# Modulation vectors by 32-column quarters of TensorE, four-block norms, and the residual affine after the first feed-forward products, in a two-block fp32 kernel

## The chip, the cores and the metric

The kernel runs on one core of one Trainium2 chip. The metric is the device time of one launch in microseconds (us), as the median of several runs. Engines are named as in the profile: PE is the matrix engine (TensorE), PEld its weight loads, DVE the vector engine, ACT the scalar engine, POOL the GpSimd engine, SP the engine that issues most transfers. `L253` is line 253 of the kernel before.

## The reference, cut to what matters

Two transformer-like blocks run one after the other on one sequence of 1024 tokens with 1024 features, all in fp32. The change touches the first block only:

```python
mod = silu(c) @ w_mod + b_mod          # 6 vectors of 1024: shift, scale, gate, twice
h   = x * (1 + scale1) + shift1        # 256 context tokens likewise, with c_ctx
y   = concat(mlstm(h), sgu(h), conv(h), s5(h)) @ w_out      # four mixers of 256 features
x1  = layer_norm(ALPHA * x + gate1 * y) * ln1_w + ln1_b
ff  = (silu(g) * u) @ w_ffn_out,  [g, u] = (x1 * (1 + scale2) + shift2) @ w_ffn_in
x2  = layer_norm(ALPHA * x1 + gate2 * ff) * ln2_w + ln2_b   # input of the second block
```

Two mixers end in a layer norm of their own over 256 features per token (the gated unit `sgu` and the convolution). The second block (attention, a state-space mixer and a linear recurrence) is the same in both kernels.

## The kernel before, in words

**Products.** Every large product is done in three passes: each fp32 operand is split into a rounded part `hi` and a rest `lo`, and hi*hi, hi*lo and lo*hi are added up in PSUM (`mm3` L237, `dense` L243, `tokens` L270). Weights come in chunks of 256 KB by `wpart` (L219): SP issues the load into `raw` (3 buffers), ACT copies `raw` to `whi` (L215), and DVE or POOL subtracts to `wlo` (L212). With a scale vector `wpart` first multiplies the chunk on DVE or POOL (L231); so is `w_out` multiplied by the gate `g0` and `w_ffn_out` by `g1`.

**Order of the work.** The kernel is written as generators that yield `(busy, wait)` estimates; `weave` (L146) runs some twenty of them side by side on a planned clock and so writes the program out in one order. Buffers come from pools of numbered slots (28 `u`, 7 `ub`, 5 `f` of 512 columns, 8 PSUM banks); `need` and `spare` make a generator wait on the planned clock until slots are free. `after(name)` waits until another generator has added that name. The tile framework then orders each engine's instructions by a timeline that it simulates itself (`schedule_with_timeline_sim=True`). At run time each engine works through its own queue in that order, and waits in a queue hold back all behind them.

**Stages of the first block.** (1) Start: `mod_part(st)` (L442) computes shift1 and scale1 for `c` and `c_ctx` in two steps, `st` 0 and 1, each for four of the eight feature blocks. Each step loads eight chunks of 512 KB of `w_mod` (L434) and multiplies them on PE with a stationary operand of 4 columns (L463, `128*4`); the chunks in `MSPLIT` are split into hi and lo first (tile `wms`), the others are used as fp32. The row of 512 sums goes to SBUF by DVE (`modrow` L469) and is turned into columns by PE (`pmt` L472). At the same time DVE builds tables for the s5 mixer (`s5_tables` L332). Then `h_split` (L482) makes the input of the projections. (2) The projections of `project` (L1363) run on PE, one after the other; beside them DVE does the 31 taps of the convolution (L823), the gates and the scans. (3) After the convolution, the other eight modulation vectors' halves are computed by `mod_part(n)` (L1300), `n` 0 and 1 for `g0`, 2 to 5 for the columns of shift2 and scale2, and 6 and 7 for `g1` after the name `wo0`. Each loads four chunks of 512 KB (L1312) and accumulates eight products of 512 columns on DVE into `macc` (L1325, L1327); PE then sums over the partitions (`pmr` L1334, or `pmb` L1342 as columns). (4) After the last projection come the second mLSTM pair, the second half of s5 in up to three streams (`s5_batch` L1133) and the norm of the convolution. (5) `out_proj` (L1451) multiplies by `w_out` in four groups of rows and halves; `norm_add` (L1501) adds the products to `res`, the residual, and takes statistics. (6) `norm1` (L1515) normalises two token blocks of 128 at a time: statistics, `rsqrt` (L292: 12 small DVE operations by Newton steps), `res` normalised in place (L1527), then `to_features` (L1479): PE transposes into PSUM, DVE scales and shifts into `hf` (L1493), ACT copies to hi and DVE subtracts to lo (L215 and L212, tile `h`). After all eight blocks, `norm1` loads `ln1` by POOL's queue and multiplies and adds it to `res` on POOL (L1548, L1549: 16 operations of 1024 columns), and names `res` done. (7) `feed_forward` (L1628) first runs three tiles of `ff_in` for the first half of the tokens, then for the second half; then tiles alternate with groups of `ff_out` (L1577), which needs the name `res`.

`ln2blocks` (L846) is the norm of two token blocks at once, with one `rsqrt` for both; `conv_norm` and `sgu_mixer` call it four times each.

Of the kernel before, what the change touches and what calls it, by code (L numbers as in the profile page):

```python
# [39 lines left out]
AFFV, LOV, SCG = 0, 2, 4  # L40
# [35 lines left out]
def tile_block(ctx: ExitStack, tc: tile.TileContext, A, out):  # L76
# [341 lines left out]
    cs = const.tile([128, 8, 4], F32, name="cs")  # L418
    s.activation(cs[:, :, 0], col("c", 0, 8), AF.Silu)
    s.activation(cs[:, :, 1], col("c_ctx", 0, 8), AF.Silu)  # L420
    v.memset(cs[:, :, 2:4], 0.0)
    cs4 = const.tile([128, 8, 4], F32R, name="cs4")
    v.tensor_copy(cs4[:, :, 0:2], cs[:, :, 0:2])
    v.tensor_tensor(cs4[:, :, 2:4], cs[:, :, 0:2], _r(cs4[:, :, 0:2]), op=ALU.subtract)
    fold = const.tile([4, 2], F32, name="fold")
    v.tensor_tensor(fold[:], ident[0:4, 0:2], ident[0:4, 2:4], op=ALU.add)
# [14 lines left out]

    def mod_part(st):  # L442
        items = [(n, q) for n in (st, 2 + st) for q in range(4)]
        todo = sorted((i + (MLAG if i in MSPLIT[st] else 0), i) for i in range(8))
        last = {i // 4: i for _, i in todo}
        pm, parts = {}, {}
        pmt = bank("pmt", (128, 8, 2))
        for pos, i in todo:
            for j in range(8):
                if j <= pos + 0.5 and j not in parts:  # L450
                    parts[j] = [wms[items[j]]]
                    if j in MSPLIT[st]:
                        yield from need(u=2)
                        parts[j] = [u("wms", (128, 2, 512), F32R) for _ in range(2)]
                        split(wms[items[j]][:], parts[j][0][:], parts[j][1][:], dve=j in MDVE[st])
                        free(wms[items[j]])
            n, q = i // 4, i % 4
            new = n not in pm
            if new:
                pm[n] = bank("pmod")  # L460
            for k in range(2):
                for x in parts[i]:
                    pe.matmul(pm[n][0:4, :], (cs4 if i in MSPLIT[st] else cs)[:, 2 * q + k, :], x[:, k, :],  # L463
                              start=new and k == 0 and x is parts[i][0],
                              stop=last[n] == i and k == 1 and x is parts[i][-1])
            free(parts[i])
            if last[n] == i:
                row = f512("modrow")
                v.tensor_copy(row[0:4, :], pm[n][0:4, :])  # L469
                free(pm[n])  # L470
                for c in range(4):
                    pe.matmul(pmt[:, 4 * n + c, :], row[0:4, c * 128:(c + 1) * 128], fold[:], start=True, stop=True)  # L472
                free(row)
            yield 0.86 if i in MSPLIT[st] else 1.72, 0.0
# [371 lines left out]
    def ln2blocks(ps_, xs, width):  # L846
        st = small("lnst", [128, 2, 6])
        mv = small("lnmv", [128, 2, 2])
        rs = small("lnrs", [128, 2])
# [4 lines left out]
        for j in range(2):  # L854
            v.tensor_scalar(xs[j], ps_[j], mv[:, j, 0:1], rs[:, j:j + 1], op0=ALU.subtract, op1=ALU.mult)

    def conv_norm():
        yield from after("cv0", "cv1", *GATE["n"])
        yield from need(u=4)
        cv = [load(f"cv{i}") for i in range(2)]  # L860
        xn = [u(f"cxn{q}", (128, 4, 256)) for q in range(2)]
        yield 0.0, 4.0
        for t in range(0, 8, 2):
            yield from need(ps=1)
            p = bank("pct", (128, 2, 256))
            for j in range(2):
                for i in range(2):
                    pe.transpose(p[:, j, i * 128:(i + 1) * 128], cv[i][:, (t + j) * 128:(t + j + 1) * 128], ident[:])
            ln2blocks([p[:, j, :] for j in range(2)], [xn[t // 4][:, t % 4 + j, :] for j in range(2)], 256)
# [192 lines left out]
    def sgu_mixer():  # L1062
# [16 lines left out]
        for t in range(0, 8, 2):  # L1079
            x = [vn[t // 4][:, t % 4 + j, :] for j in range(2)]  # L1080
            ln2blocks(x, x, 256)
            x = vn[t // 4][:, t % 4:t % 4 + 2, :]
            g.tensor_tensor(x, x, lnwb[:, 0, :].unsqueeze(1).to_broadcast([128, 2, 256]), op=ALU.mult)
            g.tensor_tensor(x, x, lnwb[:, 1, :].unsqueeze(1).to_broadcast([128, 2, 256]), op=ALU.add)
            yield 0.0, 3.0
# [214 lines left out]
    def mod_part(n):  # L1300
# [5 lines left out]
        yield from need(f=1)  # L1306
        acc = f512("macc")
        wms = []
        for q in range(5):
# [5 lines left out]
            if q:  # L1315
                wm = wms[q - 1]
                if q in MACP.get(n, ()):
                    for k in range(2):
                        s.activation(wm[:, k, :], wm[:, k, :], AF.Copy, scale=cs[:, 2 * q - 2 + k, 0:1])
                    g.tensor_tensor(wm[:, 0, :], wm[:, 0, :], wm[:, 1, :], op=ALU.add)  # L1320
                    v.tensor_tensor(acc[:], acc[:], wm[:, 0, :], op=ALU.add)
                for k in range(2) if q not in MACP.get(n, ()) else ():
                    kk = 2 * (q - 1) + k
                    if kk == 0:
                        v.tensor_scalar(acc[:], wm[:, k, :], cs[:, kk, 0:1], None, op0=ALU.mult)  # L1325
                    else:
                        v.scalar_tensor_tensor(acc[:], wm[:, k, :], cs[:, kk, 0:1], acc[:],  # L1327
                                               op0=ALU.mult, op1=ALU.add)
                free(wm)
        yield 0.0, 3.0  # L1330
# [148 lines left out]
    def to_features(xs, c0, X, hf, names, scale, bias, mul=None):  # L1479
        for d in range(0, 8, 2):  # L1480
# [5 lines left out]
            for e in range(2):  # L1486
# [28 lines left out]
    def norm1():  # L1515
        yield from after("mod")
        for un in range(4):
            if True:
                yield from after(f"wosum{un // 2 * 2 + 1}")
                mv = small("mv1", [128, 2, 2])  # L1520
                rs = small("rsd", [128, 2])
                ts = (2 * un, 2 * un + 1)
                for j, t in enumerate(ts):
                    v.bn_aggr(out=mv[:, j, :], in_=st1[:, t].rearrange("p a b -> p (a b)"))
                rsqrt(rs[:], mv[:, :, 1], 2, 1.0, LN_EPS)
                for j, t in enumerate(ts):
                    v.tensor_scalar(res[t][:], res[t][:], mv[:, j, 0:1], rs[:, j:j + 1],  # L1527
                                    op0=ALU.subtract, op1=ALU.mult)
                yield 0.0, 9.0
                hf = un // 2  # L1530
                if un % 2 == 0:
                    for d in range(8):
                        yield from need(u=1)
                        H2[d, hf] = u("h2", (128, 2, 512), F32R)
                yield from to_features([res[t] for t in ts], (un % 2) * 256, H2, hf, None,
                                       lambda d: ln1c[:, 0, d:d + 1], lambda d: ln1c[:, 1, d:d + 1])
                if un % 2:
                    done.add(f"h2{hf}")
# [7 lines left out]
        for t in range(8):  # L1546
            e = v if t < AFFV else g
# [1064 lines left out]
```

## Time and profile before

| | before |
|---|---|
| median of 3 runs | 2434.91 us (2429.49, 2434.91, 3675.43) |
| the profiled execution's own time | 2431.18 us |
| span of its profile | 2429.4 us, 29664 instructions |
| mean granted TensorE clock | 0.97 of 2.4 GHz |
| PE busy | 2258.1 us (93%) |
| DVE busy | 1314.0 us (54%) |
| POOL busy | 980.3 us (40%) |
| ACT busy | 789.0 us (32%) |

The span runs from the first to the last instruction; the 1.8 us around it are the launch. Shares of busy time are means over stages that differ much, so they are read by stretches. In a timeline row the columns are start, length, engine, line, operation, output<-inputs, shape and count; a bracket at the end gives the engine's idle time before it and what released it.

### The profile page before, as it was taken

How to read it: one execution, taken by the hardware profiler on the slowest of the kernel's cores; microseconds unless marked ns; L12 is line 12 of the kernel's file. 1: busy time of each engine (PE TensorE's matmuls, PEld its weight loads, DVE VectorE, ACT ScalarE, POOL GpSimd, SP SyncE). 2: the span in 40 equal slices, each digit the busy share in tenths (PEclk: the TensorE clock that was granted, in tenths of full speed). 3: DMA queues.
4: the chain of work that ended last, by engine and by line, in shares of the span. 5: the costliest groups of instructions: out<-in, count | busy, mean ns of one | idle time of the engine just before them, and what ended most of it. 6: DMA issues, size and time to landing. Idle time of an engine off the chain costs nothing.

```text
span 2429.4 us, 29664 instructions
## 1 busy us (share of the span) xinstructions
PE 2258.1 (93%) x10874; PEld 1795.8 (74%) x10874; DVE 1314.0 (54%) x2312; ACT 789.0 (32%) x1395; POOL 980.3 (40%) x867
## 2 busy tenths in 40 slices
PE   6888789487889999999999998999999999999998
PEld 2777677365667888888888876787777877778877
DVE  7789868897992212111121586665654666652111
ACT  2523322434232121111112245333423354543322
POOL 5455526656664223232314534123662233220543
PEclk8999989698999999999999999999999999999999
DMA  7211445235222111111111234232334433232564
GB/s 272 88 43 48 143 154 183 81 100 182 79 70 70 40 56 48 48 44 52 48 57 61 96 126 161 59 107 84 114 125 162 157 115 135 77 106 66 150 197 140
DMA packets 144194, 251.67 MB, mean 104 GB/s; under 512 B 15720, under 2 KB 51240, under 8 KB 144048
## 3 DMA queue, kind: packets, MB, share of 16 engines
q1 hardware_dynamic: 110960, 209.25, 27.1%
q10 hardware_dynamic: 30816, 32.76, 4.0%
q0 software_dynamic: 2272, 7.77, 0.9%
q8 instruction: 85, 1.39, 0.2%
q14 instruction: 61, 0.50, 0.1%
HBM read 200.20 MB, written 48.48 MB: 102 GB/s over the span
## 4 chain that ended last, share of the span: by engine, by line
PE 66%; DVE 19%; DMA 6%; issue 4%; ACT 2%; POOL 2%; SPq 0%; DVEq 0%; ACTq 0%; POOLq 0%
PE pf L251 6%; PE pf L253 6%; PE pf L255 6%; PE pz L251 6%; PE pz L253 6%; PE pz L255 6%; PE pg L239 3%; PE pg L238 3%; PE pg L240 3%; PE pO L2348 2%; PE pfo L238 2%; PE pfo L239 2%; PE pfo L240 2%; DVE cv L823 1%; DMA wm<-in_w_mod_dram 1%
## 5 line engine op out<-in xcount | busy, mean ns | idle before, releaser
L212 POOL TENSOR_TENSOR wlo<-raw,whi 128x512 fp32r<-128x512 f32 (+1 forms) x285 | 393.5, 1383 | 836.2 <-ACT whi L215 812.0
L215 ACT ACTIVATE whi<-raw 128x512 fp32r<-128x512 f32 (+1 forms) x432 | 266.8, 622 | 1019.0 <-PE pf L253 289.0
L212 DVE TENSOR_TENSOR wlo<-raw,whi 128x512 fp32r<-128x512 f32 (+1 forms) x147 | 114.9, 782 | 354.9 <-ACT whi L215 354.5
L253 PE MATMUL pf<-h,whi 128*128 128x512 f32 x704 | 234.6, 396 | 6.8 <-DVE h L212 6.8
L251 PE MATMUL pf<-h,whi 128*128 128x512 f32 x704 | 234.0, 396 | 4.8 <-ACT h L215 3.4
L255 PE MATMUL pf<-h,wlo 128*128 128x512 f32 x704 | 233.3, 395 | 2.3 <-DVE wlo L212 2.3
L251 PE MATMUL pz<-u,whi 128*128 128x512 f32 x512 | 170.6, 400 | 0.9 <-DVE sptmp L1812 0.6
L253 PE MATMUL pz<-u,whi 128*128 128x512 f32 x512 | 168.7, 395 | 0.0
L255 PE MATMUL pz<-u,wlo 128*128 128x512 f32 x512 | 166.9, 394 | 0.0
L253 PEld LDWEIGHTS pf<-h,whi 128*128 128x128 f32 x704 | 133.3, 189 | 40.3 <-DVE h L212 10.4
L251 PEld LDWEIGHTS pf<-h,whi 128*128 128x128 f32 x704 | 133.4, 190 | 35.6 <-ACT h L215 4.1
L255 PEld LDWEIGHTS pf<-h,wlo 128*128 128x128 f32 x704 | 133.3, 189 | 33.1 <-DVE wlo L212 3.4
L239 PE MATMUL pg<-wlo,act 128*128 128x512 f32 x352 | 138.3, 393 | 0.9 <-DVE wlo L212 0.7
L238 PE MATMUL pg<-whi,act 128*128 128x512 f32 x352 | 137.1, 393 | 1.8 <-ACT whi L215 1.8
L240 PE MATMUL pg<-whi,act 128*128 128x512 f32 x352 | 136.7, 391 | 0.0
L251 PEld LDWEIGHTS pz<-u,whi 128*128 128x128 f32 x512 | 96.0, 188 | 24.5 <-issue 1.9
L253 PEld LDWEIGHTS pz<-u,whi 128*128 128x128 f32 x512 | 96.3, 188 | 22.4 <-issue 1.2
L1598 DVE TENSOR_TENSOR x<-x,pg 128x512 f32<-128x512 f32 x80 | 53.6, 685 | 109.2 <-PE pg L240 109.0
L255 PEld LDWEIGHTS pz<-u,wlo 128*128 128x128 f32 x512 | 96.0, 188 | 22.0 <-issue 0.7
L1571 DVE TENSOR_TENSOR a<-a,pf 128x512 f32<-128x512 f32 x44 | 28.7, 683 | 139.8 <-PE pf L255 139.8
L239 PE MATMUL pfo<-wlo,mix 128*128 128x512 f32 x256 | 100.1, 392 | 1.4 <-POOL wlo L212 1.4
L240 PE MATMUL pfo<-whi,mix 128*128 128x512 f32 x256 | 100.1, 393 | 0.0
(647 smaller groups left out, 5108.3 us busy)
## 6 DMA issues: line engine op xcount, KB each, us to landing
raw<-in_w_ffn_in_dram SPq DMA_DIRECT2D x108, 256.0 KB
wm<-in_w_mod_dram SPq DMA_DIRECT2D x48, 512.0 KB
raw<-in_w_out_dram SPq DMA_DIRECT2D x96, 256.0 KB
raw<-in_w2f_dram SPq DMA_DIRECT2D x66, 256.0 KB
raw<-in_w_ffn_out_dram SPq DMA_DIRECT2D x56, 256.0 KB
raw<-in_w2q_dram SPq DMA_DIRECT2D x48, 256.0 KB
raw<-in_w_in_dram SPq DMA_DIRECT2D x36, 256.0 KB
mraw<-y2d SPq DMA_DIRECT2D x32, 256.0 KB
```

Of the source, the lines that this page charges most:

```text
L212: (v if dve else g).tensor_tensor(lo, full, hi, op=ALU.subtract)
L215: s.activation(hi, full, AF.Copy)
L238: pe.matmul(p, lh, rh, start=start, stop=False)
L239: pe.matmul(p, lh, rl, start=False, stop=False)
L240: pe.matmul(p, ll, rh, start=False, stop=stop)
L251: pe.matmul(p, wh, xh[k], start=k == 0, stop=False)
L253: pe.matmul(p, wh, xl[k], start=False, stop=False)
L255: pe.matmul(p, wl, xh[k], start=False, stop=k == kt - 1)
L823: v.scalar_tensor_tensor(a3, *tap(k), a3, op0=ALU.mult, op1=ALU.add)
L1571: v.tensor_tensor(a_[:], a_[:], pair[1][hf][:], op=ALU.mult)
L1598: v.tensor_tensor(x, x, p[t][:], op=ALU.add)
L2348: pe.matmul(pO[:, b, :], x[:, jb % 2, b * 128:(b + 1) * 128], H["va"][:, o:o + 96], start=False, stop=jb == nj - 1 and b == 3)
```

## The change

Five edits go together. (a) The modulation products at the start use the chunks as fp32, with no split, and 32 columns of stationary operand each: product `kk` writes partitions `32*(kk%4)` and up of one PSUM bank, so that eight products land in four quarters of 32 columns, two in each. (b) The later modulation parts do the same on PE in place of the eight DVE operations; ACT copies the bank to SBUF with a factor of 1/32. (c) `ln2blocks` becomes `lnblocks` for four token blocks, and `norm1` takes statistics and `rsqrt` for four blocks at once. (d) `to_features` with a bias does its scale and shift on ACT; the subtraction stays on DVE. (e) The multiplication and addition of `ln1` to `res` waits for the name `ffa`, which is added after the first `ff_in` of the second half, and goes half to DVE and half to POOL. The norms of the second block and `norm2` stay as they are.

```diff
@@ start: mod_part(st), L417 to L479 before @@
+    cs = const.tile([128, 23, 2], F32, name="cs")
+    s.activation(cs[:, 0:8, 0], col("c", 0, 8), AF.Silu)
+    s.activation(cs[:, 0:8, 1], col("c_ctx", 0, 8), AF.Silu)
+    v.memset(cs[:, 8:23, :], 0.0)
+    fold = const.tile([128, 2], F32, name="fold")
+    v.tensor_reduce(fold[:], ident[:].rearrange("p (q m) -> p m q", q=4)[:, 0:2, :], axis=AX.X, op=ALU.add)
...
+    def quarter(p, kk, lhs, x):
+        r0 = 32 * (kk % 4)
+        pe.matmul(p[r0:r0 + 32, :], lhs, x, start=kk < 4, stop=kk >= 4)
+
     def mod_part(st):
         pmt = bank("pmt", (128, 8, 2))
+        for n in range(2):
+            pm = bank("pmod")
+            for q in range(4):
+                x = wms[st + 2 * n, q]
+                for k in range(2):
+                    quarter(pm, 2 * q + k, cs[:, 2 * q + k:2 * q + k + 16, :].rearrange("p a b -> p (a b)"), x[:, k, :])
+                free(x)
+                yield 0.8, 0.0
+            row = f512("modrow")
+            v.tensor_copy(row[:], pm[:])
+            free(pm)
+            for c in range(4):
+                pe.matmul(pmt[:, 4 * n + c, :], row[:, c * 128:(c + 1) * 128], fold[:], start=True, stop=True)
+            free(row)
+            yield 0.8, 0.0
...
-    def ln2blocks(ps_, xs, width):
+    def lnblocks(ps_, xs):
...
-        for j in range(2):
+        for j in range(4):
             v.bn_stats(out=st[:, j, :], in_=ps_[j])
             v.bn_aggr(out=mv[:, j, :], in_=st[:, j, :])
-        rsqrt(rs[:], mv[:, :, 1], 2, 1.0, LN_EPS)
+        rsqrt(rs[:], mv[:, :, 1], 4, 1.0, LN_EPS)
...
@@ conv_norm: two steps of four blocks in two PSUM banks each, for four of two; sgu_mixer likewise @@
-            yield 0.5, 4.0
+            yield 1.0, 5.0
...
@@ mod_part(n), L1300 before @@
-        yield from need(f=1)
+        yield from need(f=1, ps=1)
         acc = f512("macc")
+        pm = bank("pmod")
...
-                        v.tensor_scalar(acc[:], wm[:, k, :], cs[:, kk, 0:1], None, op0=ALU.mult)
-                        v.scalar_tensor_tensor(acc[:], wm[:, k, :], cs[:, kk, 0:1], acc[:], op0=ALU.mult, op1=ALU.add)
+                    quarter(pm, kk, cs[:, kk, 0:1].to_broadcast([128, 32]), wm[:, k, :])
                 free(wm)
+                yield 0.8, 0.0
+        s.activation(acc[:], pm[:], AF.Copy, scale=1.0 / 32)
+        free(pm)
...
@@ to_features, with a bias @@
-                    v.tensor_scalar(x[:, 0:256], p[:, e, :], scale(d + e), bias(d + e), op0=ALU.mult, op1=ALU.add)
-                    split(x[:, 0:256], hi, lo, dve=e < LOV)
+                    s.activation(x[:, 0:256], p[:, e, :], AF.Identity, scale=scale(d + e), bias=bias(d + e))
+                    split(x[:, 0:256], hi, lo, dve=True)
...
     def norm1():
         yield from after("mod")
+        for hf in range(2):
+            yield from after(f"wosum{2 * hf + 1}")
...
+            for j in range(4):
+                v.bn_aggr(out=mv[:, j, :], in_=st1[:, 4 * hf + j].rearrange("p a b -> p (a b)"))
+            rsqrt(rs[:], mv[:, :, 1], 4, 1.0, LN_EPS)
...
+            for un in range(2):
+                ts = [4 * hf + 2 * un + j for j in range(2)]
                 for j, t in enumerate(ts):
                     v.tensor_scalar(res[t][:], res[t][:], ...)
+                yield 0.0, 9.0 if un == 0 else 0.0
+                yield from to_features([res[t] for t in ts], un * 256, H2, hf, None, ...)
+            done.add(f"h2{hf}")
+        yield from after("ffa")
         yield from need(ub=2)
...
-            e = v if t < AFFV else g
+            e = v if t % 2 else g
             e.tensor_tensor(res[t][:], res[t][:], lw[:], op=ALU.mult)
             e.tensor_tensor(res[t][:], res[t][:], lb[:], op=ALU.add)
...
     def feed_forward():
...
             for f in range(FF_FIRST):
                 yield from ff_in(f, (hf,))
+                if hf:
+                    done.add("ffa")
```

## Rows read from the trace of the kernel before

**Rows 1.** By stretch: length; busy PE, PEld, DVE, ACT, POOL; clock; DMA share, GB/s

```profile
0.00:66.00 66.00, 43.26 (x155) 18.68 (x156) 45.69 (x149) 16.75 (x30) 33.56 (x43) 0.90 0.72 257
...
40.00:66.00 26.00, 26.00 (x109) 13.66 (x109) 11.49 (x27) 8.47 (x17) 12.99 (x9) 0.89 0.37 122
...
100.00:285.00 185.00, 165.46 (x947) 140.80 (x946) 163.94 (x174) 57.30 (x106) 97.21 (x93) 0.95 0.19 61
285.00:425.00 140.00, 123.37 (x656) 99.01 (x654) 98.81 (x225) 40.02 (x82) 65.81 (x68) 0.90 0.56 174
...
577.00:640.00 63.00, 56.97 (x229) 42.04 (x228) 58.40 (x86) 18.65 (x31) 42.14 (x30) 1.00 0.43 128
640.00:740.00 100.00, 78.34 (x329) 58.78 (x328) 95.04 (x140) 29.24 (x61) 65.41 (x34) 0.92 0.19 60
740.00:1380.00 640.00, 640.00 (x2784) 522.88 (x2783) 127.71 (x192) 127.05 (x211) 196.20 (x154) 1.00 0.18 56
```

**Rows 2.** PE's longest wait, then ACT and DVE in the timeline around it

```profile
PE pmb L1342 <- ACT sp L788: 23.2, 1, 23.2
...
442.12 0.83 ACT L1153 ACTIVATE s5b<-s5a,cvec 128x640 f32<-128x640 f32 x1 [6.12 <-DVE s5a L304]
...
432.81 8.14 DVE L303 TENSOR_SCALAR s5b<-s5a 128x640 f32<-128x640 f32 x1
```

**Rows 3.** Groups of instructions by line, 640 to 740 us, DVE then POOL

```profile
L212 DVE TENSOR_TENSOR h<-hf,h 128x256 fp32r<-128x256 f32 x32 | 45.6, 1453 | 2.3 <-ACT h L215 2.3
L1493 DVE TENSOR_SCALAR hf<-ptf,ln1c 128x256 f32<-128x256 f32 x32 | 15.9, 533 | 0.6 <-PE ptf L1485 0.6
...
L1548 POOL TENSOR_TENSOR x<-x,lw 128x1024 f32<-128x1024 f32 x8 | 20.7, 2606 | 0.0
L1549 POOL TENSOR_TENSOR x<-x,lb 128x1024 f32<-128x1024 f32 x8 | 20.4, 2560 | 0.0
```

**Rows 4.** By stretch, instructions on tile macc alone: PE, PEld, DVE, clock, DMA

```profile
285.00:430.00 145.00, 6.02 (x28) 3.79 (x28) 43.46 (x48) 0.90 0.55 170
577.00:640.00 63.00, 1.02 (x2) 0.38 (x2) 21.55 (x16) 1.00 0.43 128
```

**Rows 5.** By stretch, instructions on tile pmod alone: PE, PEld, DVE, clock, DMA

```profile
0.00:40.00 40.00, 14.74 (x32) 2.44 (x32) 1.34 (x2) 0.90 0.95 345
40.00:66.00 26.00, 13.51 (x32) 2.36 (x32) 1.36 (x2) 0.89 0.37 122
```

**Rows 6.** Timeline 28 to 39 us: POOL, DVE, PE

```profile
31.91 4.70 POOL L212 TENSOR_TENSOR wms<-wm,wms 128x1024 fp32r<-128x1024 f32 x2
...
31.91 2.37 DVE L385 TENSOR_TENSOR s5b<-s5b,scols 128x32 f32<-128x32 f32 x1
...
38.39 1.86 PE L472 MATMUL pmt<-fold,modrow 4*128 4x2 f32 x8 [8.79 <-DVE modrow L469]
```

**Rows 7.** Timeline of PE, 405 to 409 us

```profile
405.34 0.63 PE L253 MATMUL pz<-hl,whi 128*128 128x512 f32 x2
405.81 0.63 PE L255 MATMUL pz<-hh,wlo 128*128 128x512 f32 x2
406.36 1.97 PE L1096 MATMUL psg<-sw,vn 128*64 128x128 f32 x32
408.26 0.73 PE L251 MATMUL pz<-hh,whi 128*128 128x512 f32 x2
```

**Rows 8.** Chain that ended last, in order of time: start, length, what

```profile
289.87 6.97 DMA wm<-in_w_mod_dram
...
343.21 0.46 PE pst L924 x4
...
403.21 6.16 DMA wm<-in_w_mod_dram
```

**Rows 9.** Page, part 5: one of rsqrt's operations, over the span

```profile
L289 DVE TENSOR_TENSOR rs<-rs,rs 128x2 f32<-128x2 f32 (+2 forms) x84 | 27.0, 327 | 1.3
```

**Rows 10.** Timeline of ACT, 649 us

```profile
649.51 0.42 ACT L215 ACTIVATE h<-hf 128x256 fp32r<-128x256 f32 x1 [3.33 <-DVE hf L1493]
```

More of the change, by code (lines that the diff above doesn't have):

```diff
@@ L39 @@
 ORDER = "QvkqguoUzKO"
-AFFV, LOV, SCG = 0, 2, 4
+SCG = 4
 NLAT = 45
@@ L439, in tile_block @@
     modA = const.tile([128, 16, 2], F32, name="modA")
+    def quarter(p, kk, lhs, x):
+        r0 = 32 * (kk % 4)
+        pe.matmul(p[r0:r0 + 32, :], lhs, x, start=kk < 4, stop=kk >= 4)
     def mod_part(st):
[L443 to L446, printed above, removed]
         pmt = bank("pmt", (128, 8, 2))
[L448 to L474, printed above, removed]
@@ L862, in conv_norm @@
         yield 0.0, 4.0
[L863 to L866, printed above, removed]
+        for q in range(2):
+            yield from need(ps=2)
+            p = [bank("pct", (128, 2, 256)) for _ in range(2)]
+            for j in range(4):
                 for i in range(2):
-                    pe.transpose(p[:, j, i * 128:(i + 1) * 128], cv[i][:, (t + j) * 128:(t + j + 1) * 128], ident[:])
-            ln2blocks([p[:, j, :] for j in range(2)], [xn[t // 4][:, t % 4 + j, :] for j in range(2)], 256)
+                    pe.transpose(p[j // 2][:, j % 2, i * 128:(i + 1) * 128],
+                                 cv[i][:, (4 * q + j) * 128:(4 * q + j + 1) * 128], ident[:])
+            lnblocks([p[j // 2][:, j % 2, :] for j in range(4)], [xn[q][:, j, :] for j in range(4)])
             free(p)
-            yield 0.5, 4.0
+            yield 1.0, 5.0
         free(cv)
@@ L1078, in sgu_mixer @@
         yield 0.0, 5.0
[L1079 to L1085, printed above, removed]
+        for q in range(2):
+            x = [vn[q][:, j, :] for j in range(4)]
+            lnblocks(x, x)
+            for j in (0, 2):
+                x = vn[q][:, j:j + 2, :]
+                g.tensor_tensor(x, x, lnwb[:, 0, :].unsqueeze(1).to_broadcast([128, 2, 256]), op=ALU.mult)
+                g.tensor_tensor(x, x, lnwb[:, 1, :].unsqueeze(1).to_broadcast([128, 2, 256]), op=ALU.add)
+            yield 0.0, 6.0
         for i in range(2):
@@ L1316, in mod_part @@
                 wm = wms[q - 1]
[L1317 to L1322, printed above, removed]
-                    kk = 2 * (q - 1) + k
-                    if kk == 0:
-                        v.tensor_scalar(acc[:], wm[:, k, :], cs[:, kk, 0:1], None, op0=ALU.mult)
-                    else:
-                        v.scalar_tensor_tensor(acc[:], wm[:, k, :], cs[:, kk, 0:1], acc[:],
-                                               op0=ALU.mult, op1=ALU.add)
+                for k in range(2):
+                    kk = 2 * (q - 1) + k
+                    quarter(pm, kk, cs[:, kk, 0:1].to_broadcast([128, 32]), wm[:, k, :])
                 free(wm)
+                yield 0.8, 0.0
+        s.activation(acc[:], pm[:], AF.Copy, scale=1.0 / 32)
+        free(pm)
         yield 0.0, 3.0
@@ L1516, in norm1 @@
         yield from after("mod")
[L1517 to L1522, printed above, removed]
+        for hf in range(2):
+            yield from after(f"wosum{2 * hf + 1}")
+            mv = small("mv4", [128, 4, 2])
+            rs = small("rsd4", [128, 4])
+            for j in range(4):
+                v.bn_aggr(out=mv[:, j, :], in_=st1[:, 4 * hf + j].rearrange("p a b -> p (a b)"))
+            rsqrt(rs[:], mv[:, :, 1], 4, 1.0, LN_EPS)
+            for d in range(8):
+                yield from need(u=1)
+                H2[d, hf] = u("h2", (128, 2, 512), F32R)
+            for un in range(2):
+                ts = [4 * hf + 2 * un + j for j in range(2)]
                 for j, t in enumerate(ts):
[L1524 to L1527, printed above, removed]
+                    v.tensor_scalar(res[t][:], res[t][:], mv[:, 2 * un + j, 0:1], rs[:, 2 * un + j:2 * un + j + 1],
                                     op0=ALU.subtract, op1=ALU.mult)
[L1529 to L1535, printed above, removed]
+                yield 0.0, 9.0 if un == 0 else 0.0
+                yield from to_features([res[t] for t in ts], un * 256, H2, hf, None,
                                        lambda d: ln1c[:, 0, d:d + 1], lambda d: ln1c[:, 1, d:d + 1])
-                if un % 2:
-                    done.add(f"h2{hf}")
+            done.add(f"h2{hf}")
+        yield from after("ffa")
         yield from need(ub=2)
```

16 lines of the change are left out of this document (3 added, 13 removed).

## The prediction, made before the changed kernel was run

> **What bounds the kernel now.** I read the table of stretches first, then PE's waits, then the groups of instructions of the stretches in question. From 740 to 1380 us PE is busy without a gap at a clock of 1.00, and DVE has 128 us of work in 640 [rows 1]. Nothing that takes work off DVE gains there. Before 740 us PE is not the bound alone: from 0 to 66 us it is busy for 43, from 640 to 740 for 78, and in these stretches DVE is busy for 46 and 95 [rows 1]. All five edits act before 740 us, so the gain is what they take out of these gaps. PE's longest single wait, 23.2 us before `pmb` (L1342), ends at 448 us: it waits for a PSUM bank; the bank is held by a projection's result that ACT is to copy out, ACT stands behind the sine of s5 (L1153), and that waits for DVE, whose L303 took 8.14 us while POOL worked on the same stage [rows 2]. From 640 to 740 us DVE's 32 subtractions into `h` take 45.6 us, 1453 ns each for 256 columns, while POOL spends 41.1 us on the residual's `lw` and `lb` [rows 3]. The modulation sums on DVE are 43.5 us in 48 operations up to 430 us, and 21.6 us in 16 operations from 577 to 640 us [rows 4].
>
> **The start.** The products on `pmod` take PE 14.74 + 13.51 = 28.25 us in 64 instructions [rows 5]. Afterwards there are also 64 instructions (16 chunks, two products each, an fp32 product being two instructions), but neighbours write different columns of the array. The nearest row for that is `psg`: products with 64 of 128 columns, alternating between the two halves, 32 of them start within 408.26 - 406.36 = 1.90 us, 0.059 us each for 128 moving columns [rows 7]. `pst`, with the full width and 130 moving columns, starts one per 0.46 / 4 = 0.115 us [rows 8]. So two column groups run side by side, at a factor of 1.9. In a chunk the two instructions of a product share a quarter, so I count two side by side, not four: an unsplit chunk of four instructions at 512 columns now takes 28.25 / 64 x 4 = 1.77 us at most and would take about 0.9. The second step then costs 7 us of PE for 13.5, and 26 of the 26 us of that stretch are PE's [rows 1], so 6.5 us come off the path. In the first step the PE waits 8.79 us for `modrow`, which stands on DVE behind the s5 tables; one of these, of 32 columns, took 2.37 us just as POOL began the 4.70 us of splitting `wms` [rows 6]. That split is gone: I take 6.5 us of the 8.79. Together -13. Bounds: -6.5 if DVE's tables are late as before, -25 if the two steps close up behind the loads (8.79 waited, 13.5 saved on PE, and the rest from DVE). What follows, up to 285 us, is bound by DVE, busy for 164 of 185 us [rows 1]; it holds nothing that the change touches, so it moves forward as a whole.
>
> The Trainium skill, "TensorEngine Tiling (Array Packing)", section Key Properties, says against this edit that a change of the tiling mode drains TensorE, and each of the 48 chunks changes it twice. By the trace the way in cost 406.36 - 405.81 = 0.55 us where the pair before took 0.47 [rows 7], so 0.08 us; with the way out counted alike, 32 chunks of the later parts lose 5 us in all. If the drain were a full matmul's 0.63 us each way, it would be 40 us; that is rival 5, and the row speaks against it.
>
> **The later modulation, 285 to 448 us.** Six parts leave DVE (48 operations, 43.5 us [rows 4]) and come to PE: 6 parts x 16 instructions x 0.23 = 22 us by half of the 0.44 us per instruction [rows 5], and 24 changes of width at 0.16 = 4 us, so 26 us. PE's gaps in 285 to 425 us are 140 - 123 = 17 us [rows 1]. A chunk can use them only when its load is there, and now the PE queue stands still when it is not: behind the quarters stand the projections. I let two thirds be hidden: +8. Bounds: 0, and +26 with nothing hidden, plus what loads make late (a rival below). ACT's copy of the bank takes the place of DVE's last operation, at about its length. DVE's 43.5 us lay beside PE's projections; that DVE is freer shows in the next term.
>
> The gap of 23.2 us at 425 us is an accident of queues, and all its links change: DVE no longer has the last part's sums ahead of the s5 work, and the bank of `pmb` follows another holder. But the three s5 streams start there together as before, with the same POOL work. Ends: 0 and -23; no row decides between them, so I take the middle, -12.
>
> **Norms of four blocks.** Six `rsqrt` fall away, four in the mixers and two in `norm1`. Each is 12 operations; one of them took 327 ns on average [rows 9], so about 4 us at most, and 3 in a quiet queue. Four in the mixers are 12 us of DVE beside PE's work; a quarter on the path: -3. Bounds 0 and -12. The two in `norm1` go with the next term.
>
> **640 to 740 us.** DVE loses 15.9 us of `hf` [rows 3], six us of `rsqrt`, and the delay of the subtractions. Their own length, were POOL quiet, I take from ACT's copy of the same 256 columns, 0.42 us [rows 10]: 32 x (1.453 - 0.42) = 33 us. So 55 of DVE's 95 us go, and ACT gets 32 x 0.42 = 13 us to its 29. PE becomes the bound: its 78 us, plus a few us at the start of the norm that no work covers (the first transposes wait for statistics, `rsqrt` and normalisation). I take -18 of the 22 us of gap [rows 1]. Bounds: -8 if POOL's subtractions `wlo` still hold DVE up, -22 if PE is filled. The tail of the output projection before it, 577 to 640 us, has PE busy for 57 of 63 us [rows 1]; DVE loses 21.6 us [rows 4] and PE gains two parts, 32 x 0.23 + 8 x 0.16 = 9 us. Gap and addition are alike: 0, bounds -6 and +9.
>
> **The residual's affine in the feed-forward.** 16 operations of 1024 columns, eight on POOL at 2.6 us, eight on DVE at no more than that [rows 3], so 21 us on each; and the two loads of `ln1`, which go through POOL's queue, and the scaling of both by ALPHA on DVE. They are due before the first `ff_out`: after the first `ff_in` of the second half come two more single and two double tiles, some 66 us of PE at 11 us per single one (48 instructions at 0.23). DVE is busy a fifth of that stage, POOL a third [rows 1]. So 0. If the cover failed, `wlo` behind two affine operations would come 5 us late; that is the upper bound, +5.
>
> **Sum.** -13 + 8 - 12 - 3 - 18 + 0 + 0 = -38 us against the profiled execution's 2431.2 us: 2393 us. The median shown, 2434.9, is 3.7 us above that execution; I leave this as noise.
>
> **Rivals.** (1) The gap stays or moves: the projections end, three s5 streams and the norm of the convolution begin, and DVE is held by POOL just as now. For: rows 2 have nothing of the modulation in their chain but `pmb` itself. Against: the order is made anew. Time: 2393 + 12 = 2405. (2) More closes up: start -25, the added PE work lies in gaps (0), gap -23, tail -22, norms -3: -73, 2358. For: nothing forbids each; against: all at once, with a PE that has only so much idle time. (3) The quarters do not overlap, and the change doesn't do what it says on PE: start -6.5, the six parts 96 x 0.44 = 42 + 4, less 17 of gaps: +29, gap -12, norms -3, tail -18: -10.5, 2421. Against: rows 7. (4) Slower: PE waits for the loads. In the chain there are six waits for a `wm` chunk between 290 and 409 us, the first 6.97 and the last 6.16 us, and 30 us in all [rows 8]. On DVE they held up side work; at the head of PE's queue they hold up projections. With all 30 us on PE, its 26 us uncovered and the gap as now: -13 + 26 + 30 - 3 - 18 = +22, 2453. It is slower than before from 8 us of waiting, a third of a us for each of 24 chunks, if nothing is hidden and the gap stays. Against: `pmr` already stands in PE's queue behind these loads, and the planner places it where PE barely waits. (5) Each change of width costs the length of a matmul: 64 changes in the later parts at 0.63 us [rows 7] instead of 0.08, none hidden: 2393 + 35 = 2428.
>
> **How the numbers follow.** Forecast 0.46, its own range 2378 to 2408; gap stays 0.24; closing up 0.15; no overlap 0.06; PE behind loads 0.06; changes of width 0.03. The range runs from 2355, just under rival 2, to 2431, the time before: above it lies rival 4, below it little. Faster by over 2% (about what a measurement of this kernel can tell from no change) means under 2386: most of rival 2 and a quarter of the forecast, 0.27. Slower by over 2% would need 2483, past rival 4: 0.01. Within 2%: 0.72.
>
> **What would show it.** Start: `pmod` at half its 28 us of PE, no `wms`, the first `h_split` some 13 us earlier than 65. Later parts: about 0.9 us of PE per chunk in four instructions; waits of PE for `wm` of a few us in sum. The gap: whether PE still has a stretch of over 15 us without an instruction after the last projection. Tail: subtractions into `h` at 0.4 to 0.7 us, PE's share from 640 us on above 95%, `lw` and `lb` beside a full PE. The prediction is wrong if PE waits over 15 us for `wm`, if the quarters run one by one, or if the time goes below 2360.

## The result, and the profile after

The changed kernel takes 2400.19 us (median of four runs, 2398.13 to 2402.67), the kernel before 2432.2 beside it: a ratio of 0.9873, 95% interval 0.9852 to 0.9894, so 1.3% faster. The profiled execution took 2402.67 us with a span of 2400.8. The forecast was 2393, 38 us below the profiled execution of the kernel before; measured were 28.5 us between the two profiled executions and 32 between the medians.

Where the time went is seen best at points of the work that both traces have (us from the span's start):

| point | before | after | difference |
|---|---|---|---|
| first tap of the convolutions (DVE) | 154.3 | 144.8 | -9.5 |
| last product of the projections (`pz`) | 422.1 | 431.4 | +9.3 |
| first product of the output projection (`po`) | 520.2 | 513.2 | -7.0 |
| first addition of `norm_add` (`x<-x,po`) | 605.1 | 587.7 | -17.4 |
| first product of the feed-forward (`pf`) | 674.6 | 658.0 | -16.6 |
| first product of its output (`pg`) | 811.1 | 780.4 | -30.7 |
| span | 2429.4 | 2400.8 | -28.6 |

The output projection's first group is added earlier, from 516.6 us on (524.5 before); `norm_add` adds the last group of each half of the tokens and takes the statistics. So the start gained 9.5, the projections lost 18.8, the stretch from there to the first `po` gained 16.3, the output projection up to `norm_add` 10.4, the stretch from the first `pf` to the first `pg` 14.1, and the feed-forward stayed full. The table of stretches after, columns as in [rows 1]:

```profile
0.00:45.00 45.00, 25.39 (x120) 11.28 (x120) 33.79 (x142) 6.99 (x18) 16.81 (x36) 0.89 0.95 351
...
275.00:345.00 70.00, 53.29 (x257) 37.22 (x259) 22.07 (x60) 18.41 (x35) 23.69 (x35) 0.80 0.49 154
345.00:432.00 87.00, 87.00 (x509) 63.77 (x505) 52.05 (x130) 27.82 (x58) 46.52 (x41) 1.00 0.55 174
432.00:460.00 28.00, 15.25 (x73) 11.00 (x66) 20.13 (x31) 20.51 (x47) 24.70 (x35) 0.63 0.30 95
...
658.00:710.00 52.00, 47.04 (x208) 37.25 (x209) 41.04 (x61) 26.42 (x55) 32.58 (x19) 0.97 0.27 86
710.00:780.00 70.00, 70.00 (x307) 57.20 (x306) 9.43 (x14) 16.78 (x28) 25.23 (x20) 1.00 0.22 68
780.00:1348.00 568.00, 568.00 (x2481) 465.37 (x2480) 117.61 (x179) 109.13 (x181) 169.51 (x132) 1.00 0.18 55
```

Three things are to be seen. The start now has its DMA busy for 0.95 of 45 us at 351 GB/s. From 275 to 345 us PE idles for 16.7 us at a mean clock of 0.80, and from 345 to 432 it has no gap at all. From 710 us on PE is busy without a gap, and nothing can be gained there but PE work. The residual's affine is not in that stretch: all its sixteen operations ran between 635.6 and 694.0 us, the first of them 22 us ahead of the first `pf`, although the program writes them behind the name `ffa`. The order in which the generators wrote them is not the order in which they ran. By first and last start:

```profile
L1529 POOL TENSOR_TENSOR x<-x,lw x4: 2388/2896/3367, 635.6 to 683.5; 128x1024 f32<-128x1024 f32 x4
L1529 DVE TENSOR_TENSOR x<-x,lw x4: 1212/1652/3419, 638.8 to 691.3; 128x1024 f32<-128x1024 f32 x4
L1530 POOL TENSOR_TENSOR x<-x,lb x4: 2403/2458/2477, 638.7 to 687.0; 128x1024 f32<-128x1024 f32 x4
L1530 DVE TENSOR_TENSOR x<-x,lb x4: 1210/1213/3426, 648.4 to 692.7; 128x1024 f32<-128x1024 f32 x4
```

So edit (e) did not put the affine under the feed-forward's full PE; it gave half of it to DVE.

The start in PE's timeline, to be read against [rows 6]; in brackets what it waited for:

```profile
11.05 5.47 PE L442 MATMUL pmod<-wm,cs 128*32 128x512 f32 x16 [11.05 <-DVE s5t L321]
18.34 1.05 PE L458 MATMUL pmt<-fold,modrow 128*128 128x2 f32 x8 [1.81 <-DVE modrow L455]
19.32 2.59 PE L442 MATMUL pmod<-wm,cs 128*32 128x512 f32 x16
26.02 1.87 PE L458 MATMUL pmt<-fold,modrow 128*128 128x2 f32 x8 [4.11 <-DVE modrow L455]
...
38.18 1.92 PE L442 MATMUL pmod<-wm,cs 128*32 128x512 f32 x16
```

Sixteen instructions take 1.92 us, 0.12 us each, where the mean was 0.44 before [rows 5]; the wait for `modrow` is 4.11 us for 8.79.

PE's waits from 275 to 650 us (total, times, longest), against [rows 2]:

```profile
PE py L1231 <- POOL s5f L1220: 7.2, 2, 6.1
PE pmod L442 <- DMA wm<-in_w_mod_dram: 6.5, 3, 3.6
PE pst L911 <- ACT sp L774: 5.8, 1, 5.8
PE pmb L1325 <- ACT macc L1311: 4.3, 1, 4.3
```

The wait of 23.2 us is gone. Behind the last projection two smaller ones stand in its place (`pmb` and `pst`). Ahead of it PE now waits 6.5 us for the chunks' loads and 7.2 us for an s5 product (`py`) that waits for POOL. The groups of the norm, 623 to 710 us, against [rows 3]:

```profile
L212 DVE TENSOR_TENSOR h<-hf,h 128x256 fp32r<-128x256 f32 x32 | 25.2, 818 | 2.0 <-ACT h L215 2.0
L1476 ACT ACTIVATE hf<-ptf,ln1c 128x256 f32<-128x256 f32 x32 | 16.9, 560 | 18.4 <-DVE h L212 16.8 <-PE ptf L1468 1.4
...
L1529 POOL TENSOR_TENSOR x<-x,lw 128x1024 f32<-128x1024 f32 x4 | 11.5, 2887 | 0.2 <-PE ptf L1468 0.2
L1530 POOL TENSOR_TENSOR x<-x,lb 128x1024 f32<-128x1024 f32 x4 | 9.8, 2449 | 0.9 <-DVE lb L1526 0.7
```

`h` fell from 45.6 to 25.2 us. All of `lw` and `lb` still lies in this stretch, but POOL's part fell from 41.1 to 21.3 us.

### The profile page after: what moved, and what is told of

Its sections match the earlier page's. It is cut to its first block, busy times and chain, and to the rows that moved or that the text cites. A ratio compares the mean times of both kernels' runs of the same rounds, so it can differ in the third digit from the quotient of the medians.

```text
span 2400.8 us, 29770 instructions
## 1 busy us (share of the span) xinstructions
PE 2260.8 (94%) x11002; PEld 1795.4 (75%) x11002; DVE 1217.6 (51%) x2148; ACT 795.5 (33%) x1425; POOL 945.5 (39%) x855
## 4 chain that ended last, share of the span: by engine, by line
PE 69%; DVE 15%; DMA 5%; issue 3%; POOL 3%; ACT 3%; SPq 1%; DVEq 0%; ACTq 0%; POOLq 0%
PE pf L255 6%; PE pf L251 6%; PE pf L253 6%; PE pz L251 6%; PE pz L253 6%; PE pz L255 6%; PE pg L238 3%; PE pg L239 3%; PE pg L240 3%; PE pO L2331 2%; DVE cv L809 2%; PE pfo L238 2%; PE pfo L239 2%; PE pfo L240 2%; PE pyd L1951 1%
## 5 line engine op out<-in xcount | busy, mean ns | idle before, releaser
L238 PE MATMUL pg<-whi,act 128*128 128x512 f32 x352 | 137.1, 393 | 0.4 <-ACT whi L215 0.4
```

The costliest lines, as they stand in the source:

```text
L238: pe.matmul(p, lh, rh, start=start, stop=False)
```

## The experiments

All ratios are against the kernel before; the changed kernel's is 0.9873. Two ratios differ by more than their noise from about 0.0026 on, 6 us (the root of the two half-widths squared and summed).

**x1: the start alone**, in the kernel before; `cs`, `fold`, `quarter` and the start's `mod_part` are those of the change.

```diff
-    cs = const.tile([128, 8, 4], F32, name="cs")
+    cs = const.tile([128, 23, 2], F32, name="cs")
...
+    def quarter(p, kk, lhs, x):
...
```

> The kernel before, with the start's modulation alone by column quarters (and the wider cs and fold that it needs). In the changed kernel the convolution's first product comes 9.5 us earlier. Theory A, the convolution's DVE work carries this through: about 9 us less than before, 2423. Rival B, the time is given back where the projections meet the s5 streams: 0 to -3 us, about 2431. Rival C, the stall at 425 to 448 us turns out otherwise by the shift alone: -20 us or more, under 2413. In all three the products on pmod start one per 0.12 us where their loads are there.

Measured: 2421.85 us, ratio 0.9953 (0.9935 to 0.9971), -11 us. Theory A holds (about 2423), and the stall is still there, in PE's waits:

```profile
PE pmb L1328 <- ACT sp L774: 23.4, 1, 23.4
```

So a shift by itself does not break up the queues at 425 us.

**x2: the later sums back on DVE.**

```diff
-                    quarter(pm, kk, cs[:, kk, 0:1].to_broadcast([128, 32]), wm[:, k, :])
+                    v.scalar_tensor_tensor(acc[:], wm[:, k, :], cs[:, kk, 0:1], acc[:],
+                                           op0=ALU.mult, op1=ALU.add)
```

> The changed kernel with the later modulation's sums back on DVE (macc), all else as changed. Between 285 and 431 us the changed kernel lost 18.7 us against the one before, and between its last projection and the output projection it won 27. Theory A, both come from this edit, net -8: undone it takes 2408 us. Rival B, only the loss comes from it and the stall was closed by the other edits: 2400 - 19 = 2381. Rival C, only the gain comes from it (the loss is of the new order of loads, whatever engine sums): 2427. What the last projection's time and the stall ahead of pmb look like tells them apart.

Measured: 2401.82 us, ratio 0.9872 (0.9855 to 0.9889): the same time as changed. Its waits and its stretch up to 432 us:

```profile
PE pmb L1330 <- ACT sp L774: 23.4, 1, 23.4
```

```profile
345.00:432.00 87.00, 66.22 (x404) 54.16 (x403) 72.55 (x130) 28.61 (x57) 52.63 (x47) 0.88 0.48 156
```

The last projection comes at 410.2 us instead of 431.4, PE then stands 23.4 us, the first `po` is at 504.6 instead of 513.2, and `norm_add`'s first addition at 584.4 instead of 587.7. The edit does both, loss and closing, and they cancel: theory A's mechanism with a net of 0, not -8. In this stretch PE's busy time is 66 of 87 us for 87, because the 23.4 us lie in it, and DVE's is 73 for 52.

**x3 and x4: the affine without its wait and all on POOL; `hf` back on DVE.**

```diff
-        yield from after("ffa")
-            e = v if t % 2 else g
+            e = g
```

> The changed kernel with the residual's affine back right behind the norm, all sixteen operations on POOL. Between the output projection's end and the first feed-forward output the changed kernel is 14 us shorter. Theory A, POOL's affine slowed the subtractions into h (45.6 us before, 25.2 after): 10 to 14 us slower than changed, 2410 to 2414, h back over 1.2 us each. Rival B, DVE was late because of its own 16 us of hf: 0 to 4 us, 2400 to 2404, although h is slow again.

```diff
-                    s.activation(x[:, 0:256], p[:, e, :], AF.Identity, scale=scale(d + e), bias=bias(d + e))
+                    v.tensor_scalar(x[:, 0:256], p[:, e, :], scale(d + e), bias(d + e), op0=ALU.mult, op1=ALU.add)
```

> The changed kernel with the input affine hf of the feed-forward's norm back on DVE (some 16 us there, 17 us off ACT). Theory A, with POOL's affine out of the way DVE has room: 0 to 4 us slower, 2400 to 2404. Rival B, DVE's 16 us stand on the chain from the norm to the first products: 10 to 14 us slower, 2410 to 2414.

Measured: 2410.29 us, 0.9917 (0.9892 to 0.9942), and 2405.46, 0.9887 (0.9867 to 0.9908). From `norm_add`'s first addition to the first `pg` it is 206.0 us before, 192.7 changed, 201.9 in x3 and 197.1 in x4: undoing the affine's edit costs 9.2 and undoing ACT's `hf` 4.4, about the 13.3 that the two kernels differ by. The groups of x3 (623 to 720 us), then of x4:

```profile
L212 DVE TENSOR_TENSOR h<-hf,h 128x256 fp32r<-128x256 f32 x32 | 40.1, 1303 | 5.1 <-ACT h L215 5.1
L1528 POOL TENSOR_TENSOR x<-x,lw 128x1024 f32<-128x1024 f32 x8 | 20.3, 2553 | 0.1
```

```profile
L212 DVE TENSOR_TENSOR h<-hf,h 128x256 fp32r<-128x256 f32 x32 | 29.7, 955 | 0.0
...
L1476 DVE TENSOR_SCALAR hf<-ptf,ln1c 128x256 f32<-128x256 f32 x32 | 16.1, 531 | 0.3 <-PE ptf L1468 0.3
```

With all of the residual's affine on POOL, `h` takes 1303 ns again although DVE has no `hf`. Theory A holds in x3, but the affine's place is not what differs: it starts at 634.7 us there and at 635.6 in the changed kernel. What differs is POOL's share, sixteen operations for eight. The single subtractions bear it out. Before, 21 of the 32 ran beside one of POOL's `lw` or `lb` and took 1.93 us on average; changed, 7 did, at 1.98; in x3, 17, at 2.09. With POOL idle they take 0.40 to 0.42 us in all three. In x4 the end lies between the theories (about 4 us by the points, not to be told from 0 by the ratios).

**x5: norms of two blocks**, in `conv_norm`, the gating mixer and `norm1`.

```diff
-    def lnblocks(ps_, xs):
-        rsqrt(rs[:], mv[:, :, 1], 4, 1.0, LN_EPS)
+    def ln2blocks(ps_, xs, width):
+        rsqrt(rs[:], mv[:, :, 1], 2, 1.0, LN_EPS)
...
```

> The changed kernel with the norms of two blocks at once again (four more inverse square roots in the mixers, two more in the norm ahead of the feed-forward), the affine left where the change put it. Theory A, only the operations themselves count: 0 to 4 us slower, 2400 to 2404. Rival B, with pairs the norm's first transposes start earlier (two blocks' statistics instead of four), so it is up to 5 us faster. Rival C, their wait sits between DVE and PE at the norm and costs 5 us or more.

Measured: 2414.33 us, 0.9932 (0.9918 to 0.9947): 14 us slower than changed, a miss of theories A and B. C has the size (5 us or more) but not the place: it named the norm ahead of the feed-forward, and from `norm_add`'s first addition to the first `pg` it is 194.0 us, only 1.3 more than changed. The loss lies ahead of that: `norm_add`'s first addition is 12.0 us late (599.7 for 587.7), and the first `po` 23.5 us (536.7 for 513.2). The convolution's norm by first and last start of its transposes and its normalisations; changed, then x5:

```profile
L854 PE MATMUL pct<-ident,lcv x16: 272/273/421, 480.0 to 505.7; 128*128 128x128 f32 x16
L841 DVE TENSOR_SCALAR cxn<-pct,lnmv,lnrs x8: 531/535/544, 500.8 to 515.8; 128x256 f32<-128x256 f32 x8
```

```profile
L854 PE MATMUL pct<-ident,lcv x16: 272/273/273, 502.6 to 528.6; 128*128 128x128 f32 x16
L841 DVE TENSOR_SCALAR cxn<-pct,lnmv,lnrs x8: 532/538/544, 514.8 to 542.2; 128x256 f32<-128x256 f32 x8
```

From the first transpose to the last normalisation it is 36 us with four blocks a round and 40 with two. Each round is a trip from PE's transposes through DVE's statistics and its twelve operations of `rsqrt`, with other streams' work between, but these rounds account for only 4 us here: 22.6 of the 26 us by which the norm ends later are there before its first transpose. The other norm that the edit touches, in the gating mixer, is not late (last `vn` normalisation at 359.6 us for 360.5). With the sums on DVE the same stretch is 61 us with two blocks (x1) and 30 with four (x2), and yet the first `po` comes at the same time in both. So the norm's length alone does not set that point. Whether the delay of x5 comes from the norms or from the order that the planner then makes is not shown.

The four combinations that now exist (all with the new start) give `norm_add`'s first addition, one execution each, with the first `po` in brackets:

| | norms of two | norms of four |
|---|---|---|
| sums on DVE | x1: 590.1 (505.2) | x2: 584.4 (504.6) |
| sums on PE | x5: 599.7 (536.7) | changed: 587.7 (513.2) |

What differs behind this point (affine, `hf`) does not reach it: x3 has 586.4 and x4 590.1, which is also how far two kernels can be apart here that differ only behind it. At this point the norms win 6 to 12 us and the sums on PE lose 3 to 10. At the first `po` the norms win 1 to 24 and the sums lose 9 to 32, so these sizes depend on the point.

**x6 and x6b: the later sums in the convolution's stretch.**

```diff
-"d": seq(after("cv1", *GATE["d"]), mod_gate(0), mod_cols())
+"d": seq(after(*GATE["d"]), mod_gate(0), mod_cols())
```

In x6b `after("cv0")` stands in its place.

> The changed kernel, with the later modulation's parts started at once instead of behind the second convolution (one wait less in the planner's list; the sums stay on PE). With the sums on DVE (x2) the last projection ended at 410 us and PE stood 23.4 us; with them on PE it ended at 431 and PE stood 5.8 + 4.3 us; the time was the same. Theory A, what was gained in the stall was paid as PE work and lower clock ahead of it, so with that work in the convolution's stretch, where PE has gaps and the DMA is busy for a tenth, both are had: last projection at about 415, no wait over 10 us, 10 to 18 us faster than changed, 2382 to 2390. Rival B, the stall's end is set by the s5 streams whatever PE did: the wait is 20 us again and the time stays at 2400. Rival C, the loads take buffers from the convolution's streams: slower than 2405.

> As x6_mod_early, but started behind the first of the two convolutions, so with the later half of that stretch. Theory A: the same gain if six parts fit there, 2382 to 2392; rival B: 2400; rival C, buffers: if x6 is slow for want of buffers, this one is less so.

Measured: 2418.28 us, 0.9954 (0.994 to 0.9968), and 2419.52, 0.995 (0.9932 to 0.9967): 19 to 20 us slower than changed. A fails, and so does B. C has the sign in x6, but by C the later start of x6b should have cost less, and it did not (0.995 for 0.9954). The convolution's stretch and its longest wait (75 to 275 us) in x6, then the stretch in x6b:

```profile
100.00:275.00 175.00, 145.67 (x773) 113.43 (x771) 149.46 (x164) 49.28 (x99) 106.42 (x91) 0.90 0.22 71
```

```profile
PE pw L1172 <- POOL s5f L1167: 11.5, 7, 4.0
```

```profile
100.00:275.00 175.00, 160.50 (x919) 131.69 (x917) 159.70 (x169) 52.41 (x105) 102.66 (x91) 0.94 0.24 74
```

Changed, PE is busy there for 155 us at a clock of 0.96, and that wait is 0.9 us. In x6 the gaps were not free: PE did less there, not more. In x6b PE did more (160.5 us), the wait is 3.3 us, and the time is the same; the last projection is as late in both (447.6 and 446.6 us for 431.4). So neither reason covers both runs, and the cause stays open.

**x7: neighbours in one quarter.**

```diff
-        r0 = 32 * (kk % 4)
-        pe.matmul(p[r0:r0 + 32, :], lhs, x, start=kk < 4, stop=kk >= 4)
+        r0 = 32 * (kk // 2)
+        pe.matmul(p[r0:r0 + 32, :], lhs, x, start=kk % 2 == 0, stop=kk % 2 == 1)
```

> The changed kernel, but a chunk's two products go to the same quarter of the columns (quarter = product number over two), so that neighbours no longer write different columns; the same sums. Theory A, the quarters run side by side and that gives the pitch of 0.117 us per instruction (16 in 1.92 us): here 0.22 us or more, 3.5 us and more for 16, and the later parts' 64 to 96 instructions each 0.1 us longer, some 10 us of PE. Rival B, the pitch comes from the short stationary operand (32 columns for 4 before): unchanged at 0.12 us.

Measured: 2412.37 us (one run). The later chunks in PE's timeline, x7, then changed:

```profile
38.48 1.94 PE L442 MATMUL pmod<-wm,cs 128*32 128x512 f32 x16
...
373.27 1.90 PE L442 MATMUL pmod<-wm,cs 128*32 128x512 f32 x4
...
385.41 1.92 PE L442 MATMUL pmod<-wm,cs 128*32 128x512 f32 x8
```

```profile
370.19 1.05 PE L442 MATMUL pmod<-wm,cs 128*32 128x512 f32 x4
...
380.63 1.06 PE L442 MATMUL pmod<-wm,cs 128*32 128x512 f32 x8
```

One chunk (x4) takes 1.90 us in one quarter and 1.05 in two; two chunks (x8) take 1.92 in two quarters and 1.06 in four. Theory A has the mechanism: the quarters work side by side, and within one the instructions start 0.43 to 0.45 us apart. It misses where the chunks come in a row: sixteen take 1.94 us in x7 too, though the kernel writes each quarter's four together. By their single starts these sixteen come in four groups of four, each group within 0.04 us and 0.43 us behind the one ahead. So neighbours need not differ in the kernel's order; it is enough that the four quarters are loaded alike within the run.

**x9, x9b, x12: other ways to issue the same chunks; x10: the gate's two parts on DVE.**

```diff
-            if q:
+            if q in (2, 4):
...
+            if q == 4:
...
+            if q >= 3:
...
```

The first line is the changed kernel's, the next three are x9 (two chunks together), x9b (all four behind the fourth load) and x12 (one chunk, three loads behind). In x10 the parts with n < 2 use `macc` on DVE as in x2.

> The changed kernel; a later part's four chunks go to PE two at a time, so that all four quarters work in each group. In the changed kernel six of the chunks between 370 and 425 us stand alone and take 1.05 us with two quarters, as much as two chunks together (1.06). Theory A, PE's work ahead of the last projection counts one to one (x7: 10 us more there, 12 us more in all): 5 us less PE work, 2395, less what the later load makes it wait. Rival B, DVE's chain has the same length there (x2), so less PE work only lengthens the stall ahead of pmb: 2400.

> The changed kernel; a later part's four chunks go to PE in one group of sixteen instructions behind the fourth load. Same PE work as by two (1.92 us for sixteen), three buffers more held. Theory A: 2393 to 2397, and with fewer points where PE meets a load that is late, its 6.5 us of waiting for wm under 4. Rival B: 2400, the stall ahead of pmb longer. Rival C, held buffers delay other loads: slower than 2403.

> The changed kernel with the first two of the six parts (the gate's, at 288 to 345 us) summed on DVE as before and the other four on PE; the tail's parts stay on PE. DVE is busy there for 22 of 70 us, PE stood 6.5 us for wm, at a mean clock of 0.80. Theory A, PE's order is the bound up to the last projection: that comes 6 to 9 us earlier and the time is 2391 to 2396. Rival B, the stall returns as in x2: 2400. The wait ahead of pmb tells.

> The changed kernel; a later part's first three loads are issued before its first chunk goes to PE (one before in the changed kernel, four in x9b), and the chunks still go one at a time. In x9b the last projection came 28 us earlier than in the changed kernel, with only some 6 us of PE work less; PE's wait for wm fell from 6.5 to 0.5 us and its idle time between 275 and 345 us from 16.7 to 4.5. Theory A, the lead of the loads did it, PE's queue no longer stands at a load: 2384 to 2392, wait for wm under 2 us, last projection before 412 us. Rival B, the grouping did it, the chunks being fewer places in PE's queue: about 2400 here, last projection after 420 us.

| | us | ratio (95%) | last `pz` | `norm_add`'s first addition | `pz` products in 285 to 323 us |
|---|---|---|---|---|---|
| changed | 2400.19 | 0.9873 (0.9852 to 0.9894) | 431.4 | 587.7 | 14 |
| x9 by two | 2412.05 | 0.9919 (0.9897 to 0.9941) | 436.1 | 588.6 | 8 |
| x9b by four | 2387.3 | 0.9828 (0.9813 to 0.9842) | 403.6 | 573.4 | 90 |
| x12 loads ahead | 2405.48 | 0.99 (0.9883 to 0.9916) | 424.6 | 591.7 | 28 |
| x10 gate on DVE | 2402.57 | 0.9894 (0.9878 to 0.9911) | 416.7 | 585.6 | 50 |

x9's profiled execution took 2401.9 us, its three others 2411.9 to 2413.8, so its points do not explain its median, which misses both its theories (2395 and 2400). x10 misses both of its own: the last projection comes 14.7 us earlier, as A says, but the time is that of the changed kernel within the noise, and the stall of B does not come back (PE's longest wait from 275 to 650 us is 8.7 us). x9b beats both kernels, and its theory A (2393 to 2397). Its PE is busy 5.6 us less over the whole span (2255.2 for 2260.8), but its last projection is 28 us earlier, so the work is not the reason. x12 was to tell whether the loads' lead was: theory A fails there, and the numbers are rival B's (2405, last projection at 424.6). The stretch 275 to 345 us of x9b, and what SP's queue waited for from 270 us on in the changed kernel and in x9b:

```profile
275.00:345.00 70.00, 65.48 (x361) 47.87 (x361) 27.66 (x74) 24.72 (x52) 27.97 (x38) 0.95 0.59 190
```

```profile
SPq L1301 <- PE py L1231: 14.1, 2, 13.0
SPq L1301 <- PE pmod L442: 3.2, 2, 2.0
```

```profile
SPq L1301 <- PE py L1231: 3.4, 1, 3.4
```

The changed kernel's SP queue stands 13.0 us at a chunk's load (L1301), whose buffer an s5 product (`py`) still reads; behind it stand the projections' `raw` loads, four of them issued in 270 to 325 us for eight in x9b. From 285 to 323 us PE is busy in x9b for 35.6 of 38 us, 22.9 of them with the projections' products, at a clock of 0.99; changed it is 24.1 and 3.0, at 0.72. That wait is not all of it: x2 waits 11.9 us at the same place and has 57 products. Each variant gets another order from the planner; which of its choices (buffer, bank or queue) does it in x9b stays open.

## Why the prediction was right, and where it was wrong

The time and the class came out as forecast: 7 us above 2393, within 2378 to 2408. Of its seven terms two had the right size, one of these for a wrong reason; the others' errors cancelled in part, so the closeness of the sum is partly luck.

- **Start, -13: right mechanism, measured -9.5** (x1: -11). `pmod` runs faster than assumed and `wms` is gone, but the second step ends 21 us earlier only to meet a late weight: PE then stands 7.4 us for `whi` (L238), which stands on ACT behind splits of `hh` that wait for DVE's `hf` (L471). The middle priced no wait behind the second step.
- **Later modulation, +8, and the gap, -12: the step that failed is that they were summed as independent.** Measured +18.8 up to the last projection (+21.2 against x2), where the price of 26 us of PE work was too high (`pmod` is busy for 17 us there) and the hiding in gaps too hopeful: PE got idle time and a low clock instead, with 14 projection products in 285 to 323 us for 54 in the kernel before (295 to 333 us, the same place). The gap closed, by this edit alone (x1 and x2 keep 23.4 us, x3 to x5 do not have it). By x2 the two together are worth 0 us, not -4.
- **Norms of four, -3: the size is wrong, 6 to 12 us at `norm_add`, 14 in the time (x5).** I counted operations (12 us of DVE) and took a quarter for the path. The rounds between PE and DVE, which I left out, are 4 us in the convolution's norm by x5; what makes up the rest is not shown.
- **577 to 640, 0, and 640 to 740, -18: right in kind, measured +0.8 and -14.1.** The subtractions were held up by POOL's affine, as said (x3: 9.2 us), and `hf` on ACT gives some 4 by the points (x4), not told from 0 by the times. `h` came to 818 ns on average with a median of 414, my 0.42. The step that is off is "were POOL quiet": the whole affine still runs beside the norm, eight operations of it on POOL, and PE's share from 658 to 710 us is 90%, not above 95%.
- **Affine in the feed-forward, 0: the size is right, the reason is not.** I let it run under a full PE, with some 66 us of products in which to hide. It ran ahead of that, from 635.6 to 694.0 us, so this cover was never put to the test. PE's 568 of 568 us from 780 on say nothing of it.

Of the rivals, gap stays (1) and no overlap (3) fell by the rows above. Closing up (2) had part of it: x9b, at 2387 with its last projection at 403.6 us, shows that the gain of the gap can be had without the loss ahead of it. Rival 4, PE behind loads, was there in small (6.5 us at `wm`), but its larger form is in SP's queue, which I had not followed. Rival 5, a change of width at the cost of a matmul, falls by PE's timeline; first two chunks (eight instructions) behind a projection's product, then one chunk (four) ahead of one:

```profile
287.65 0.40 PE L255 MATMUL pz<-hh,wlo 128*128 128x512 f32 x1
287.97 1.06 PE L442 MATMUL pmod<-wm,cs 128*32 128x512 f32 x8
288.86 0.98 PE L1179 MATMUL pk<-s5c,scols 128*16 128x240 f32 x4
...
370.19 1.05 PE L442 MATMUL pmod<-wm,cs 128*32 128x512 f32 x4
371.18 0.74 PE L251 MATMUL pz<-hh,whi 128*128 128x512 f32 x2
```

The way in takes 0.32 us where projections follow each other at 0.23, so 0.09. Ahead of the 16 columns of `pk` the two chunks give way after 0.89 us, twice 0.44; ahead of a full-width product the chunk gives way after 0.99, so 0.1 us more. The Trainium skill ("TensorEngine Tiling (Array Packing)", Key Properties) says that a change of the tiling mode drains TensorE. By these rows that costs about 0.1 us each way here, not a matmul's 0.63.

## What to carry to other kernels

Where one engine's stall ends with another engine's chain, moving work from the chain's engine to the stalled one moves the loss: price the two as one term, and ask which end is fixed. Work that the program text moves has to be looked for in the trace before its cover is counted: here the affine ran where it had been, and what helped was that POOL had half of it. Small operations in a chain over two engines were worth more than their busy time let expect (14 us for 3); why is open here. Where a planner orders the streams, a few ways of issuing the same work spread over 25 us (2387 to 2412), so such variants are worth measuring before a mechanism is argued.

## What was not expected of the hardware

Four column quarters of fp32 products run side by side: sixteen instructions of 512 columns in four quarters take 1.92 us, and four in one quarter 1.90 (x7), so the rate is four times that of one quarter. And PE goes past a busy quarter, if its queue has the instructions in the order in which the kernel writes them (the trace shows their starts only): in x7 four instructions in a row go to the same quarter, four such groups follow each other, and all sixteen take 1.94 us, their starts four at a time within 0.04 us.
